# The gate projection of a hybrid decoder layer: 26 of 32 output tiles by seven block products, with gates and branches kept in DRAM

## The chip, the cores and the metric

The kernel runs on one core of a Trainium2 chip. The metric is the device time of one execution in microseconds; the time of a kernel is the median of its runs. The profile is that of one further execution.

## The reference

One layer of a decoder serves 512 prompt tokens and 8 sample tokens (520 in all) with shared weights; `D_MODEL` is 2048. Cut to the part that matters here:

```python
xn = rmsnorm(x, attn_norm_w)
proj = xn @ w_in                                    # q, k, v, gu, gv: 3584 columns
attn = sink_attention(...)                          # 16 heads, window 128 -> 1024 columns
sgu = gelu(gu) * spatial_mix(layernorm(gelu(gv)))   # chunks of 128 positions -> 1024 columns
branch_attn = attn @ w_br_attn                      # 1024 -> 2048
branch_sgu = sgu @ w_br_gm                          # 1024 -> 2048
gates = sigmoid(xn @ w_gate + b_gate)               # 2048 -> 4096
merged = gates[..., D_MODEL:] * branch_attn + gates[..., :D_MODEL] * branch_sgu
x = x + merged @ w_out
# then ConvFFN: up projection 2048 -> 11264, causal conv of width 3, silu gate, down projection 5632 -> 2048
# then x += sigmoid(rmsnorm(x) @ w_ple_gate) * (p @ w_ple_proj)
```

All inputs and outputs are float32.

## The kernel before, in words

Activations lie transposed: a tile holds 128 features by 520 tokens, in two halves of 260 (256 prompt tokens and 4 sample tokens each). A projection works through *n-tiles* of 128 output features; each sums over *k-tiles* of 128 input features. To keep float32 accuracy every operand is split into a rounded part `hi` and a rest `lo`, and a product is taken as hi*hi + hi*lo + lo*hi. A 128x128 block of weights (a *key* `(name, k, n)`) thus costs six matmuls of 260 columns, two halves by three parts (method `mm`).

All weights pass through one stream (`weight_stream`, class `Stream`) whose order is fixed when the program is built. Eight keys make a *block* of 128x1024 that SP loads into a tile `st` (three buffers, three blocks ahead). At the start of block v (`block_start`) ACT casts block v+2 to `hi` (L266) and DVE subtracts it to get `lo` (L273). The other work is hung onto this clock: generators in `self.bg` take one step per block (`tick`), `self.fine` takes one step per key, and `at_block` puts a function at the "snap", "act", "dve" or "end" point of a later block. Each engine runs its instructions in the order in which the program emits them.

The up projection and two of the five chunks of the down projection already use a form with fewer multiplications (`Stream.winograd`, `wpair`): two n-tiles are taken together as a 2x2 block product of (pairs of k-tiles) x (two n-tiles) with the two token halves, and seven products P1 to P7 replace eight. A pair of n-tiles over 16 k-tiles is seven blocks of eight keys, each key costing three matmuls of 260 columns: 168 matmuls for the pair, where the plain form takes 192. The sums of weight blocks are made on the way: tiles `S` and `L` (pool `wsp`) get a second block added by an accumulating DMA from POOL's queue or by DVE (L297, L299). The sums of input tiles are made by `woperands` (`tau`, `X`; ACT casts at L446, DVE subtractions at L449 and sums at L435 to L441), and the seven products are put together again from PSUM with four copies on ACT (L390) and four operations on DVE (L394, L398, L402, L403). In PSUM a phase is either two pairs of banks plus four single banks (plain) or eight single banks (seven products, four for each pair of n-tiles).

Around the change the order is: `front` (normalised input `xn`, input projection, attention on the side), then `gates`, then `w_out`. In `gates` the first loop takes, for each of 16 n-tiles, the attention half of the gate (96 matmuls), multiplies by the row scale `R`, applies the sigmoid, then takes the attention branch `bra` (48 matmuls) and multiplies. Meanwhile the gMLP generator `gmlp` runs one step per block: the GELUs that were left over (L1116), transposes of `gv` (L1154), statistics and scaling per token chunk (L1141 to L1160), the triangular mix of eight channel tiles (L1170 to L1190, matmuls at L1180 and L1181), and last the sample rows (L1194 to L1216, matmuls `gx` at L1211). The second loop takes the other gate half and the branch `brg`, adds, and splits the result into `mg` for `w_out`. `xn` is held as 16 pairs of tiles (hi, lo), each over both token halves. Main storage is a pool of 67 slots of 128x538 floats (`slot`), with a few more slots in phase pools (`extra`).

Of the kernel before, what the change touches and what calls it, by code (L numbers as in the profile page):

```python
# [34 lines left out]
EPS = 1e-6  # L35
SLOT = 538
NSLOT = 67
EARLY_MG = 6
OUT_GROUP = 3
BLK = 8  # L40

# [8 lines left out]
PRODUCTS = ("P1", "P5", "P6", "P2", "P4", "P7", "P3")  # L50
BANK = {"P5": "b", "P1": "a", "P2": "c", "P6": "a", "P4": "d", "P7": "a", "P3": "b"}
KQ = KD // 2

SLOPES = np.exp2(-8.0 * np.arange(1, NH + 1, dtype=np.float32) / np.float32(NH)).astype(np.float32)

# [28 lines left out]
class Stream:  # L84
# [28 lines left out]
    def winograd(self, name, n1, n2, ks):  # L113
        assert not self.open and len(ks) % 2 == 0 and len(ks) <= 2 * BLK
        v = len(self.keys)
        r11, r21, r22, r12 = (self.block([(name, k, n) for k in kk])
                              for kk, n in ((ks[0::2], n1), (ks[0::2], n2), (ks[1::2], n2), (ks[1::2], n1)))
        for p in PRODUCTS:
            self.vblock([(name, p, n1, i) for i in range(len(ks) // 2)],
                        {"P1": ("L", r11), "P7": ("L", r11), "P2": ("st", r12), "P4": ("st", r22)}.get(p, ("S", r21)))  # L120
        acts = self.acts
        acts[v - 6].append(("load", "L", r11, r11))
        acts[v - 1] += [("vsum", "S", r21, ("L", r11)), ("sum", "L", r11, r21)]
        if name == "up":
            acts[v - 9].append(("load", "S", r21, r21))
            acts[v - 8].append(("sum", "S", r21, r22))
            acts[v - 4].append(("load", "st", r12, r12))
            acts[v - 2].append(("load", "st", r22, r22))
            acts[v].append(("vsum", "S", r21, ("st", r12)))
        else:  # L130
            acts[v - 7].append(("load", "S", r21, r21))
            acts[v - 5].append(("load", "st", r22, r22))
            acts[v - 3] += [("vsum", "S", r21, ("st", r22)), ("load", "st", r12, r12)]
            acts[v].append(("vsum", "S", r21, ("st", r12)))
# [8 lines left out]
def weight_stream():  # L143
    o = Stream()
    o.add(paired("in", K_TILES[0], K_TILES[1], KD))
    for n in V_TILES + MIX_TILES:
        o.nt("in", n, range(KD))
    for n in range(KD):
        o.nt("gate", KD + n, range(KD))
        o.nt("bra", n, range(KG))  # L150
    for n in range(KD):
        o.nt("gate", n, range(KD))
        o.nt("brg", n, range(KG))
    for n in range(KD - OUT_GROUP):
        o.nt("out", n, range(KD))
    o.add(grouped("out", range(KD - OUT_GROUP, KD), KD))
    for n in range(KD):
        o.nt("pproj", n, range(KP))
    for j in range(KF):
        o.winograd("up", j, KF + j, range(KD))  # L160
    for c, ks in enumerate(ff_chunks()):
        for n in range(0, KD, 2):
            if seven(c):
                o.winograd("down", n, n + 1, ks)
            else:
                for m in (n, n + 1):
                    o.nt("down", m, ks)
    for n in range(KD):
        o.nt("pgate", n, range(KD))
    return o.done()  # L170
# [13 lines left out]
NCV = _c  # L184


class Kernel:
    def __init__(self, ctx, tc, a):
        self.tc = tc
        self.nc = tc.nc  # L190
        self.a = a
        self.ctx = ctx
        nc = self.nc
        self.stp = ctx.enter_context(tc.tile_pool(name="stp", bufs=3))
        self.sp = ctx.enter_context(tc.tile_pool(name="sp", bufs=NSLOT))
        self.cp = ctx.enter_context(tc.tile_pool(name="cp", bufs=1))
        self.smp = ctx.enter_context(tc.tile_pool(name="smp", bufs=2))
        self.drp = ctx.enter_context(tc.tile_pool(name="drp", bufs=1, space=bass.MemoryType.DRAM))
        self.x1d = [self.drp.tile([128, NT], F32, name=f"x1d{n}") for n in range(KD)]
        self.ppd = [self.drp.tile([128, NT], F32, name=f"ppd{n}") for n in range(KD)]  # L200
        self.fd = [self.drp.tile([128, NT], F32, name=f"fd{j}") for j in range(KF)]
        self.pos = 0
        self.st = {}
        self.hi = {}
        self.lo = {}
        self.bg = []
        self.uid = 0
        self.fine = iter(())
        self.late = defaultdict(list)
        self.slotp = {}  # L210
# [139 lines left out]

    def mm(self, ps, key, x, start, stop):
        whi, wlo = self.wtile(key)
        xh, xl = self.v2(x[0]), self.v2(x[1])
        mm = self.nc.tensor.matmul
        for h in range(2):
            mm(ps[:, h, 0:HW], lhsT=whi, rhs=xh[:, h, :], start=start, stop=False)  # L356
        for h in range(2):
            mm(ps[:, h, 0:HW], lhsT=whi, rhs=xl[:, h, :], start=False, stop=False)  # L358
        for h in range(2):
            mm(ps[:, h, 0:HW], lhsT=wlo, rhs=xh[:, h, :], start=False, stop=stop)  # L360

    def ntile(self, name, n, ks, xs):
        ps = self.mmps()
# [105 lines left out]
    def split(self, src_v, name, scale=None):  # L469
# [9 lines left out]
                                           op0=ALU.mult, op1=ALU.subtract)  # L479
        return hi, lo  # L480

    def rsqrt_rows(self, pss, out, factor, quick=False):

        nc = self.nc
        slow = [] if quick else [None]
        v, y, t = self.slot(name="rv"), self.slot(name="ry"), self.slot(name="rt")
        for h in range(2):
            nc.vector.tensor_scalar(out=v[:, h * HW:(h + 1) * HW], in0=pss[h], scalar1=factor, scalar2=EPS,
                                    op0=ALU.mult, op1=ALU.add)
        nc.vector.reciprocal(y[:, 0:HW], v[:, 0:HW])  # L490
# [46 lines left out]
    def run(self):  # L537
# [40 lines left out]
        with ExitStack() as c1:  # L578
            self.psum(c1, 2, 4)
            with ExitStack() as c2:  # L580
                self.atp = self.phase(c2, "atp")
                self.extra(c2, 8, "s0", "s1", "kT", "sv")
                self.front(x)
            with ExitStack() as c2:
                self.gmp = self.phase(c2, "gmp")
                self.extra(c2, 8, "wt", "nw", "wm", "gnh", "gnl", "mx", "mgx")
                self.gates()
        with ExitStack() as c2:
            self.wsp = self.phase(c2, "wsp", 2)
            with ExitStack() as c1:  # L590
# [19 lines left out]
    def front(self, x):  # L610
# [5 lines left out]
        ps = [self.mmps(), self.mmps()]  # L616

        def xsplit(*ks):
            xn.extend(self.split(self.v2(x[k]), "xn", scale=self.col("an", k)) for k in ks)

        xsplit(0)
        self.split_block(0, (0, 2))
# [65 lines left out]
        self.drain(g4)  # L688
        self.drain(g2)

    def gates(self):
        nc, a, xn = self.nc, self.a, self.xn
        g3 = self.gmlp()
        next(g3)
        self.bg.append(g3)
        merged = []
        for n in range(KD):
            p = self.ntile("gate", KD + n, range(KD), xn)
            m = self.slot(name="mgx" if n < 2 or n >= 10 else "mg")
            nc.vector.tensor_mul(self.v2(m), self.pv(p), self.v2(self.R))  # L700
            nc.scalar.activation(m[:, 0:NT], m[:, 0:NT], AF.Sigmoid, bias=self.col("bg", KD + n))
            p = self.ntile("bra", n, range(KG), self.at)
            nc.vector.tensor_mul(self.v2(m), self.pv(p), self.v2(m))
            merged.append(m)
        self.drain(g3)
        self.sg = [self.split(self.v2(z), "sg") for z in self.gu]
        self.mg = {}
        for n in range(KD):
            p = self.ntile("gate", n, range(KD), xn)
            g = self.slot(name="g")  # L710
            nc.vector.tensor_mul(self.v2(g), self.pv(p), self.v2(self.R))
            nc.scalar.activation(g[:, 0:NT], g[:, 0:NT], AF.Sigmoid, bias=self.col("bg", n))
            if n == KD - 1:
                self.fine = self.split_each(merged, self.mg, EARLY_MG, KD, "mg")
            p = self.ntile("brg", n, range(KG), self.sg)
            nc.vector.tensor_mul(self.v2(g), self.pv(p), self.v2(g))
            nc.vector.tensor_add(merged[n][:, 0:NT], merged[n][:, 0:NT], g[:, 0:NT])
            if n < EARLY_MG:
                self.mg[n] = self.split(self.v2(merged[n]), "mg")
        self.xn = self.sg = None  # L720

    def norm1(self, x):
        nc = self.nc
# [917 lines left out]
```

## Time and profile before

| | |
|---|---|
| median of 3 runs | 2725.32 us (2725.3 to 2725.63) |
| profiled execution | 2725.98 us |
| span of its profile | 2724.3 us, 53560 instructions |
| PE busy | 2707.0 us (99%), 22524 matmuls |
| DVE busy | 1749.6 us (64%) |
| ACT busy | 1196.2 us (44%) |
| POOL busy | 260.7 us (10%) |
| DMA | 390.33 MB, mean 143 GB/s |
| mean granted TensorE clock | 0.999 |

The span is the time from the first to the last instruction of the profiled execution. PE is TensorE's matmuls, DVE is VectorE, ACT ScalarE, POOL GpSimd, SP the engine that issues most transfers. A row of the timeline reads: start, duration, engine, line, operation, output <- inputs, shapes, count, and in brackets how long the engine was idle before it and what released it. A row of the groups by line reads: line, engine, operation, output <- inputs, shapes, count, then busy us and mean ns, then idle time before and its releasers. A row of waits reads: us in total, times, longest. A row of the chain of work that ended last reads: start, duration, piece. Matmuls are pipelined: one is shown with some 280 ns, while they start some 120 ns apart.

### The profile page before, as it was taken

To read this page: it belongs to the slowest core of one execution; us is meant where nothing else is said; L and a number is where in the kernel's file an instruction comes from. 1 tells how busy PE (TensorE), PEld (TensorE's weight loads), DVE (VectorE), ACT (ScalarE), POOL (GpSimd) and SP (SyncE) were. 2 spreads that over 40 slices of the span, in tenths; PEclk is the share of its full clock that TensorE was granted. 3 is DMA by queue.
4 is the path that set the end of the run, shared out by engine and by line. 5 is a ranking of instruction groups with operands and counts; after the bars stand their busy time and mean duration, and the time that the engine had idled before them with its cause. 6 is when DMAs were issued, how large, how long until landed. Compare 5 with 4: busy or idle time off the path is not lost.

```text
span 2724.3 us, 53560 instructions
## 1 busy us (share of the span) xinstructions
PE 2707.0 (99%) x22524; PEld 2703.2 (99%) x22524; DVE 1749.6 (64%) x2594; ACT 1196.2 (44%) x1996; POOL 260.7 (10%) x417
## 2 busy tenths in 40 slices
PE   9999999999999999999999999999999999999999
PEld 9999999999999999999999999999999999999999
DVE  5666555442433343678888888888888677576533
ACT  5365452221322233465555555555556445444321
POOL 0111000000000000011111111111111111110000
PEclk9999999999999999999999999999999999999999
DMA  5223323222222344576666666666658667776343
GB/s 187 92 81 101 102 83 98 89 89 94 88 92 93 94 135 136 162 213 163 178 175 161 177 167 174 172 164 175 173 157 242 158 176 208 158 180 185 112 141 106
DMA packets 129618, 390.33 MB, mean 143 GB/s; under 512 B 14736, under 2 KB 15888, under 8 KB 129376
## 3 DMA queue, kind: packets, MB, share of 16 engines
q1 hardware_dynamic: 101376, 307.75, 34.4%
q0 software_dynamic: 25696, 74.90, 15.6%
q8 instruction: 176, 2.88, 0.4%
q10 hardware_dynamic: 2304, 4.26, 0.4%
q14 instruction: 66, 0.54, 0.1%
HBM read 340.43 MB, written 46.42 MB: 142 GB/s over the span
## 4 chain that ended last, share of the span: by engine, by line
PE 98%; ACT 1%; DVE 1%; DMA 0%; issue 0%; ACTq 0%; SPq 0%; DVEq 0%
PE wa L417 18%; PE mm L356 18%; PE mm L360 18%; PE mm L358 18%; PE wb L417 12%; PE wd L417 6%; PE wc L417 6%; PE po L966 1%; PE s L903 1%; PE pt L948 0%; PE pl L1514 0%; ACT hi L266 0%; DMA ppd<-pp 0%; PE qss L775 0%; ACT pp L1287 0%
## 5 line engine op out<-in xcount | busy, mean ns | idle before, releaser
L273 DVE TENSOR_TENSOR lo<-st,hi 128x1024 fp32r<-128x1024 f32 (+3 forms) x378 | 453.7, 1201 | 376.2 <-ACT hi L266 375.5
L266 ACT CAST hi<-st 128x1024 fp32r<-128x1024 f32 (+3 forms) x378 | 389.6, 1031 | 386.0 <-PE mm L358 149.4
L417 PE MATMUL wa<-X,hi 128*128 128x260 f32 x2736 | 500.6, 283 | 0.9 <-ACT pp L1287 0.9
L417 PEld LDWEIGHTS wa<-X,hi 128*128 128x128 f32 x2736 | 420.8, 188 | 1.1 <-ACT pp L1287 1.1
L356 PE MATMUL mm<-xnh,hi 128*128 128x260 f32 x1920 | 393.9, 287 | 5.6 <-ACT hi L266 5.6
L360 PE MATMUL mm<-xnh,lo 128*128 128x260 f32 x1920 | 386.4, 283 | 0.0
L358 PE MATMUL mm<-xnl,hi 128*128 128x260 f32 x1920 | 386.3, 282 | 0.0
L417 PE MATMUL wa<-X,lo 128*128 128x260 f32 x1368 | 385.7, 282 | 0.0
L417 PE MATMUL wb<-X,hi 128*128 128x260 f32 x1824 | 332.9, 283 | 0.0
L356 PEld LDWEIGHTS mm<-xnh,hi 128*128 128x128 f32 x1920 | 295.4, 189 | 5.7 <-ACT hi L266 5.6
L358 PEld LDWEIGHTS mm<-xnl,hi 128*128 128x128 f32 x1920 | 299.4, 190 | 0.0
L360 PEld LDWEIGHTS mm<-xnh,lo 128*128 128x128 f32 x1920 | 293.5, 188 | 0.0
L417 PEld LDWEIGHTS wb<-X,hi 128*128 128x128 f32 x1824 | 280.5, 188 | 0.0
L266 ACT CAST hi<-S 128x1024 fp32r<-128x1024 f32 (+2 forms) x180 | 181.7, 1009 | 184.5 <-DVE S L299 140.2
L273 DVE TENSOR_TENSOR lo<-S,hi 128x1024 fp32r<-128x1024 f32 (+2 forms) x180 | 210.8, 1171 | 78.5 <-ACT hi L266 78.2
L417 PEld LDWEIGHTS wa<-X,lo 128*128 128x128 f32 x1368 | 257.6, 188 | 0.0
L417 PE MATMUL wb<-X,lo 128*128 128x260 f32 x912 | 256.9, 282 | 0.0
L273 DVE TENSOR_TENSOR lo<-L,hi 128x1024 fp32r<-128x1024 f32 (+2 forms) x120 | 140.7, 1173 | 88.2 <-ACT hi L266 84.2
L417 PEld LDWEIGHTS wb<-X,lo 128*128 128x128 f32 x912 | 172.1, 189 | 0.0
L417 PE MATMUL wc<-X,hi 128*128 128x260 f32 x912 | 166.6, 283 | 0.0
L417 PE MATMUL wd<-X,hi 128*128 128x260 f32 x912 | 166.5, 283 | 0.0
L266 ACT CAST hi<-L 128x1024 fp32r<-128x1024 f32 (+2 forms) x120 | 121.2, 1010 | 100.2 <-PE wd L417 95.5
(297 smaller groups left out, 5246.4 us busy)
## 6 DMA issues: line engine op xcount, KB each, us to landing
st<-in_w SPq DMA_DIRECT2D x343, 512.0 KB, 3.9
S<-in_w SPq DMA_DIRECT2D x44, 512.0 KB, 3.5
S<-in_w POOLq DMA_DIRECT2D x44, 512.0 KB, 7.7
L<-in_w SPq DMA_DIRECT2D x44, 512.0 KB, 3.9
L<-in_w POOLq DMA_DIRECT2D x44, 512.0 KB, 5.5
fd<-hb SPq DMA_DIRECT2D x44, 260.0 KB, 2.2
fr<-fd SPq DMA_DIRECT2D x44, 260.0 KB, 4.9
x1d<-dn POOLq DMA_DIRECT2D x32, 260.0 KB, 5.8
```

The costliest lines, as they stand in the source:

```text
L266: self.nc.scalar.copy(self.hi[v][:, c], self.st[WS.src[v]][:, c])
L273: self.nc.vector.tensor_sub(self.lo[v][:, c], self.st[WS.src[v]][:, c], self.hi[v][:, c].bitcast(F32))
L356: mm(ps[:, h, 0:HW], lhsT=whi, rhs=xh[:, h, :], start=start, stop=False)
L358: mm(ps[:, h, 0:HW], lhsT=whi, rhs=xl[:, h, :], start=False, stop=False)
L360: mm(ps[:, h, 0:HW], lhsT=wlo, rhs=xh[:, h, :], start=False, stop=stop)
L417: nc.tensor.matmul(ps(z), lhsT=w, rhs=x, start=new and i == 0 and q == 0, stop=i == len(X[p]) - 1 and q == 2, skip_group_check=True)
L903: nc.tensor.matmul(out, lhsT=self.cols(q, c), rhs=keys(kk, c), start=n == 0, stop=n == 1)
L966: nc.tensor.matmul(po[:, kb * 128:kb * 128 + w], lhsT=vv[:, kb * 128:(kb + 1) * 128], rhs=pp[:, o:o + w], start=kb == 0 and n == 0, stop=k ...
```

## The change

The stage becomes four:

1. `branch_attn`: the attention branch first, all 16 n-tiles, copied to DRAM (`ad`, issued by ACT). The gMLP generator now runs beside it through `self.fine`, one step every three keys (`paced`). The gMLP's result `gu` is then written to DRAM (`gud`).
2. `gates_plain`: six gate n-tiles in the plain form. Meanwhile `x` is loaded again, scaled, and the operands P4 to P7 of the seven products are built; P1, P2 and P3 use the tiles of `xn` as they are, since `xn` is now split by token halves (`split_halves`, class `Halves`: each tile holds hi and lo of one half).
3. `gates_seven`: the other 26 gate n-tiles as 13 pairs by `wpair`. `gate_end` applies `R`, the sigmoid and, for the attention half, the product with the branch read back from DRAM (`av`), and writes the tile to DRAM (`gd`). During the last pair `gu` is read back and split.
4. `branch_gm`: the gMLP branch, 16 n-tiles; each reads back its two gate tiles, multiplies, adds and splits to `mg`.

```diff
-EARLY_MG = 6
+PLAIN_GATES = 6
+GATE_TILES = tuple(range(KD, 2 * KD)) + tuple(range(KD))
...
-        if name == "up":
+        if name != "down":
...
     for n in range(KD):
-        o.nt("gate", KD + n, range(KD))
         o.nt("bra", n, range(KG))
+    for n in GATE_TILES[:PLAIN_GATES]:
+        o.nt("gate", n, range(KD))
+    for n in range(PLAIN_GATES, 2 * KD, 2):
+        o.winograd("gate", GATE_TILES[n], GATE_TILES[n + 1], range(KD))
     for n in range(KD):
-        o.nt("gate", n, range(KD))
         o.nt("brg", n, range(KG))
...
     def mm(self, ps, key, x, start, stop):
         whi, wlo = self.wtile(key)
-        xh, xl = self.v2(x[0]), self.v2(x[1])
+        if isinstance(x, Halves):
+            xh, xl = [t[:, 0:HW] for t in x.t], [t[:, HW:NT] for t in x.t]
+        else:
+            xh, xl = ([self.v2(t)[:, h, :] for h in range(2)] for t in x)
...
+    def split_halves(self, src, name, scale):
+        nc = self.nc
+        t = [self.slot(F32R, name) for _ in range(2)]
+        for h in range(2):
+            nc.scalar.activation(t[h][:, 0:HW], src[:, h * HW:(h + 1) * HW], AF.Copy, scale=scale)
+        for h in range(2):
+            nc.vector.scalar_tensor_tensor(out=t[h][:, HW:NT], in0=src[:, h * HW:(h + 1) * HW], scalar=scale,
+                                           in1=t[h][:, 0:HW].bitcast(F32), op0=ALU.mult, op1=ALU.subtract)
+        return Halves(t)
...
-    def gates(self):
...
+    def branch_attn(self):
+        nc = self.nc
+        g3 = self.gmlp()
+        next(g3)
+        def paced():
+            for _ in g3:
+                yield
+                yield
+                yield
+        self.fine = paced()
         for n in range(KD):
             p = self.ntile("bra", n, range(KG), self.at)
+            t = self.slot(name="ae")
+            nc.scalar.copy(self.v2(t), self.pv(p))
+            nc.scalar.dma_start(self.ad[n], t[:, 0:NT])
+        self.at = None
+        self.finish_fine()
+        for d in range(KG):
+            nc.sync.dma_start(self.gud[d], self.gu[d][:, 0:NT])
+    def gate_end(self, n, t, b):
...
+        if attn:
+            av = self.slot(name="av")
+            nc.sync.dma_start(av[:, 0:NT], self.ad[i - KD])
+        self.at_block(b, times_r, "dve")
+        self.at_block(b + 1, sigmoid, "act")
+        if attn:
+            self.at_block(b + 2, times_a, "dve")
+        self.at_block(b + 3, lambda: nc.sync.dma_start(self.gd[n], t[:, 0:NT]))
+    def gates_plain(self):
...
+        def run():
+            for i in range(KQ):
+                for k in (2 * i, 2 * i + 1):
+                    xb[k] = self.slot(name="xr")
+                    nc.sync.dma_start(xb[k][:, 0:NT], a["x"][k])
+                yield
+                yield
+                yield
+                yield
+                for k in (2 * i, 2 * i + 1):
+                    nc.scalar.activation(xb[k][:, 0:NT], xb[k][:, 0:NT], AF.Copy, scale=self.col("an", k))
+                yield from build([(p, i) for p in ("P5", "P6", "P4", "P7")], 1)
+        self.fine = run()
+        for n in range(PLAIN_GATES):
+            p = self.ntile("gate", GATE_TILES[n], range(KD), xn)
+            t = self.slot(name="gv")
+            nc.scalar.copy(self.v2(t), self.pv(p))
+            self.gate_end(n, t, 0)
+    def gates_seven(self):
...
+        for n in range(PLAIN_GATES, 2 * KD, 2):
+            if n == 2 * KD - 2:
+                self.fine = sg_parts()
+            c = self.wpair("gate", GATE_TILES[n], GATE_TILES[n + 1], self.X)
+            self.gate_end(n, c["c1"], 1)
+            self.gate_end(n + 1, c["c2"], 2)
+    def branch_gm(self):
...
+        for n in range(KD):
+            load(n + 2)
             p = self.ntile("brg", n, range(KG), self.sg)
+            m, g = gm.pop(n), gg.pop(n)
             nc.vector.tensor_mul(self.v2(g), self.pv(p), self.v2(g))
+            nc.vector.tensor_add(m[:, 0:NT], m[:, 0:NT], g[:, 0:NT])
+            self.mg[n] = self.split(self.v2(m), "mg")
```

More of the change, by code (lines that the diff above doesn't have):

```diff
@@ L184, with __init__ @@
 NCV = _c
+class Halves:
+    def __init__(self, t):
+        self.t = t
 class Kernel:
@@ L199, in __init__ @@
         self.x1d = [self.drp.tile([128, NT], F32, name=f"x1d{n}") for n in range(KD)]
+        self.ad = [self.drp.tile([128, NT], F32, name=f"ad{n}") for n in range(KD)]
+        self.gd = [self.drp.tile([128, NT], F32, name=f"gd{n}") for n in range(2 * KD)]
+        self.gud = [self.drp.tile([128, NT], F32, name=f"gud{n}") for n in range(KG)]
         self.ppd = [self.drp.tile([128, NT], F32, name=f"ppd{n}") for n in range(KD)]
@@ L352, in mm @@
         whi, wlo = self.wtile(key)
-        xh, xl = self.v2(x[0]), self.v2(x[1])
+        if isinstance(x, Halves):
+            xh, xl = [t[:, 0:HW] for t in x.t], [t[:, HW:NT] for t in x.t]
+        else:
+            xh, xl = ([self.v2(t)[:, h, :] for h in range(2)] for t in x)
         mm = self.nc.tensor.matmul
         for h in range(2):
-            mm(ps[:, h, 0:HW], lhsT=whi, rhs=xh[:, h, :], start=start, stop=False)
+            mm(ps[:, h, 0:HW], lhsT=whi, rhs=xh[h], start=start, stop=False)
         for h in range(2):
-            mm(ps[:, h, 0:HW], lhsT=whi, rhs=xl[:, h, :], start=False, stop=False)
+            mm(ps[:, h, 0:HW], lhsT=whi, rhs=xl[h], start=False, stop=False)
         for h in range(2):
-            mm(ps[:, h, 0:HW], lhsT=wlo, rhs=xh[:, h, :], start=False, stop=stop)
+            mm(ps[:, h, 0:HW], lhsT=wlo, rhs=xh[h], start=False, stop=stop)
     def ntile(self, name, n, ks, xs):
@@ L585, in run @@
                 self.gmp = self.phase(c2, "gmp")
-                self.extra(c2, 8, "wt", "nw", "wm", "gnh", "gnl", "mx", "mgx")
-                self.gates()
+                self.extra(c2, 8, "wt", "nw", "wm", "gnh", "gnl", "mx", "ae")
+                self.branch_attn()
+            c2 = ExitStack()
+            self.wsp = self.phase(c2, "wsp", 2)
+            self.extra(c2, 4, "xr", "tau")
+            self.gates_plain()
+        with ExitStack() as c1:
+            self.psum(c1, 0, 8)
+            self.gates_seven()
+        c2.close()
+        self.slotp = {}
+        with ExitStack() as c1:
+            self.psum(c1, 2, 4)
+            self.branch_gm()
         with ExitStack() as c2:
@@ L618, in xsplit @@
         def xsplit(*ks):
-            xn.extend(self.split(self.v2(x[k]), "xn", scale=self.col("an", k)) for k in ks)
+            xn.extend(self.split_halves(x[k], "xn", self.col("an", k)) for k in ks)
         xsplit(0)
@@ L689, in front @@
         self.drain(g2)
-    def gates(self):
-        nc, a, xn = self.nc, self.a, self.xn
+    def branch_attn(self):
+        nc = self.nc
         g3 = self.gmlp()
         next(g3)
-        self.bg.append(g3)
-        merged = []
+        def paced():
[4 more added lines that the diff above has]
+        self.fine = paced()
         for n in range(KD):
[L698 to L701, printed above, removed]
@@ L702, in gates @@
             p = self.ntile("bra", n, range(KG), self.at)
[L703 to L706, printed above, removed]
+            t = self.slot(name="ae")
[5 more added lines that the diff above has]
+            nc.sync.dma_start(self.gud[d], self.gu[d][:, 0:NT])
@@ new lines, in branch_attn, with times_r, sigmoid, times_a @@
+        self.gu = None
+        self.zt = None
+    def gate_end(self, n, t, b):
+        nc = self.nc
+        i = GATE_TILES[n]
+        attn = i >= KD
+        def times_r():
+            nc.vector.tensor_mul(t[:, 0:NT], t[:, 0:NT], self.R[:, 0:NT])
+        def sigmoid():
+            nc.scalar.activation(t[:, 0:NT], t[:, 0:NT], AF.Sigmoid, bias=self.col("bg", i))
+        def times_a():
+            nc.vector.tensor_mul(t[:, 0:NT], t[:, 0:NT], av[:, 0:NT])
+        if attn:
[6 more added lines that the diff above has]
+        self.at_block(b + 3, lambda: nc.sync.dma_start(self.gd[n], t[:, 0:NT]))
@@ new lines, in gates_plain @@
+    def gates_plain(self):
+        nc, a, xn = self.nc, self.a, self.xn
+        X = {p: [None] * KQ for p in PRODUCTS}
+        for i in range(KQ):
+            X["P1"][i] = xn[2 * i].t[0]
+            X["P2"][i], X["P3"][i] = xn[2 * i + 1].t
+        xb = {}
+        self.X, build = self.woperands(xb)
+        self.X.update(X)
+        def run():
+            for i in range(KQ):
+                for k in (2 * i, 2 * i + 1):
[8 more added lines that the diff above has]
+                yield from build([(p, i) for p in ("P5", "P6", "P4", "P7")], 1)
+                del xb[2 * i], xb[2 * i + 1]
+        self.fine = run()
[4 more added lines that the diff above has]
+            self.gate_end(n, t, 0)
+        self.finish_fine()
+        self.xn = None
@@ new lines, in gates_seven, with sg_parts @@
+    def gates_seven(self):
+        nc = self.nc
+        self.sg = {}
+        def sg_parts():
+            raw = {}
+            for d in range(KG + 1):
+                if d < KG:
+                    raw[d] = self.slot(name="gu")
+                    nc.sync.dma_start(raw[d][:, 0:NT], self.gud[d])
+                for _ in range(5):
+                    yield
+                if d:
+                    self.sg[d - 1] = self.split(self.v2(raw.pop(d - 1)), "sg")
+        for n in range(PLAIN_GATES, 2 * KD, 2):
[4 more added lines that the diff above has]
+            self.gate_end(n + 1, c["c2"], 2)
+        self.X = None
+        self.finish_fine()
+        for kind in ("snap", "act", "dve", "end"):
+            self.run_late(kind, self.now())
@@ L707, in gates, with load @@
+    def branch_gm(self):
+        nc = self.nc
+        gm, gg = {}, {}
+        def load(n):
+            if n < KD:
+                for z, i in ((gm, n), (gg, KD + n)):
+                    z[n] = self.slot(name="ml")
+                    nc.sync.dma_start(z[n][:, 0:NT], self.gd[i])
         self.mg = {}
+        load(0)
+        load(1)
         for n in range(KD):
-            p = self.ntile("gate", n, range(KD), xn)
-            g = self.slot(name="g")
-            nc.vector.tensor_mul(self.v2(g), self.pv(p), self.v2(self.R))
@@ L712, in gates @@
-            nc.scalar.activation(g[:, 0:NT], g[:, 0:NT], AF.Sigmoid, bias=self.col("bg", n))
-            if n == KD - 1:
-                self.fine = self.split_each(merged, self.mg, EARLY_MG, KD, "mg")
+            load(n + 2)
             p = self.ntile("brg", n, range(KG), self.sg)
+            m, g = gm.pop(n), gg.pop(n)
             nc.vector.tensor_mul(self.v2(g), self.pv(p), self.v2(g))
-            nc.vector.tensor_add(merged[n][:, 0:NT], merged[n][:, 0:NT], g[:, 0:NT])
-            if n < EARLY_MG:
-                self.mg[n] = self.split(self.v2(merged[n]), "mg")
@@ L720, in gates @@
-        self.xn = self.sg = None
+            nc.vector.tensor_add(m[:, 0:NT], m[:, 0:NT], g[:, 0:NT])
+            self.mg[n] = self.split(self.v2(m), "mg")
+        self.sg = None
     def norm1(self, x):
```

## The prediction, made before the changed kernel was run

> **What bounds the kernel now.** I read the page's first part, then the chain of work that ended last: TensorE carries 98% of it.
>
> ```profile
> span 2724.3 us, 53560 instructions
> PE 2707.0 (99%) x22524; PEld 2703.2 (99%) x22524; DVE 1749.6 (64%) x2594; ACT 1196.2 (44%) x1996; POOL 260.7 (10%) x417
> PE 98%; ACT 1%; DVE 1%; DMA 0%; issue 0%; ACTq 0%; SPq 0%; DVEq 0%
> ```
>
> Then what TensorE waited for in the whole run; these rows are most of it, and 5.6 us of the first is the start:
>
> ```profile
> PE mm L356 <- ACT hi L266: 6.6, 2, 5.6
> PE mm L356 <- ACT pp L1287: 2.0, 3, 0.9
> PE mm L356 <- DVE c L402: 0.6, 1, 0.6
> ```
>
> So time goes with the count of matmuls unless a new wait appears. Busy time by stretch gives the price of one (columns: PE, PEld, DVE, ACT, POOL busy, PEclk, DMA share, GB/s):
>
> ```profile
> 690.00:966.00 276.00, 276.00 (x2302) 276.00 (x2301) 101.39 (x112) 67.90 (x79) 0.00 (x0) 1.00 0.31 96
> ...
> 1235.78:1255.90 20.12, 20.12 (x170) 20.12 (x169) 17.30 (x24) 10.84 (x19) 3.20 (x6) 1.00 0.64 170
> ```
>
> The first is the second gate half with its branch: 16 x (96 + 48) = 2304 matmuls in 276.0 us, 0.1198 us each. The second is one pair of n-tiles by seven products in the up projection. The chain dates a pair by its first block:
>
> ```profile
> 1238.10 2.89 PE wa L417 x24
> ...
> 1258.24 2.89 PE wa L417 x24
> ```
>
> 20.14 us for 7 x 8 x 3 = 168 matmuls, 0.1199 us each: the seven-product form runs at the same rate, TensorE without a gap, at full granted clock. DVE is 17.3 of 20.1 us busy there, so it has room, but little.
>
> **The change part by part.**
>
> *Matmuls (-37.2).* 26 n-tiles leave the plain form: 26 x 96 x 0.1198 = 299.0 us. 13 pairs come: 13 x 20.14 = 261.8 us. The six plain gate tiles, both branches and the gMLP's small matmuls keep their counts. The Trainium skill, "TensorE: Matmul & The Clock Gate", section "Back-to-back issue gap", gives a warm isolated gap of N/2.4 + 2.5 ns; with N = 260 that is 110.8 ns by that page, an estimate that would make this term 312 x 0.1108 = 34.6. The trace disagrees by 9 ns for each matmul, and the trace decides.
>
> *Is the seven-product stage fed?* Groups by line, shapes apart (count, busy us, mean ns):
>
> ```profile
> L273 DVE TENSOR_TENSOR lo<-S,hi 128x1024 fp32r<-128x1024 f32 x132 | 161.6, 1224 | 49.0 <-ACT hi L266 48.9
> L299 DVE TENSOR_TENSOR S<-S,st 128x1024 f32<-128x1024 f32 x44 | 54.2, 1231 | 1.5
> L402 DVE TENSOR_TENSOR c<-wb,un 128x260 f32<-128x260 f32 x60 | 25.3, 421 | 0.0
> L700 DVE TENSOR_TENSOR mg<-mm,R 128x520 f32<-128x520 f32 x8 | 5.6, 700 | 28.4 <-PE mm L360 28.4
> ```
>
> A pair costs DVE seven rests at 1.22, two block sums at 1.23, four combinations at 0.42 and, at most, four products at 0.70 (R and the branch, two tiles): 15.5 us, against 17.3 in the up pair. ACT is below 11. Weight traffic is that of an up pair, 170 GB/s at a DMA share of 0.64; instead of one 266 KB write there are two writes and up to two reads, so about 210 GB/s, share about 0.79. No added wait: I take 0.
>
> *The gMLP mix beside the attention branch alone (+7.6).* Today the generator `gmlp` takes one step per block of 5.76 us. Now `paced` takes one every three keys, 3 x 0.72 = 2.16 us. These rows of today's timeline (PE, ACT, DVE, POOL, and one of the chain) give the chain of work:
>
> ```profile
> 395.34 0.41 PE L356 MATMUL mm<-xnh,hi 128*128 128x260 f32 x2
> ...
> 395.43 8.56 ACT L1116 ACTIVATE z<-z 128x520 f32<-128x520 f32 x16
> 403.88 2.00 ACT L266 CAST hi<-st 128x1024 fp32r<-128x1024 f32 x2
> ...
> 396.15 3.08 DVE L1107 TENSOR_TENSOR al<-ov,ah 64x8 fp32r<-64x8 f32 x16
> 404.95 2.36 DVE L273 TENSOR_TENSOR lo<-st,hi 128x1024 fp32r<-128x1024 f32 x2 [5.72 <-ACT hi L266]
> 407.23 0.69 DVE L1136 TENSOR_TENSOR whl<-wm,whl 128x512 fp32r<-128x512 f32 x1
> 407.83 1.29 DVE L1141 BATCH_NORM_STATS2 sm<-g 128x6 f32<-128x512 f32 x2
> 409.40 0.15 DVE L1145 TENSOR_SCALAR sm<-sm 128x1 f32<-128x1 f32 x1
> 413.04 2.64 DVE L1158 TENSOR_SCALAR z<-g,sm,sm 128x128 f32<-128x128 f32 x8
> ...
> 409.64 0.58 POOL L1147 TENSOR_TENSOR sm<-sm,mhalf 128x1 f32<-128x1 f32 x1 [5.43 <-DVE sm L1145]
> ...
> 401.26 0.87 PE g L1154 x8
> ```
>
> Sixteen GELUs hold ACT to 404.0, so DVE's next rest starts at about 405.0 whatever comes behind it. Then, back to back: rest to 406.2, mask rest to 406.85, and per token chunk 1.3 (statistics) + 0.35 + 0.65 (power on POOL) + 2.64 (eight scalings) = 4.9 us, four times; three rests fall among them (1.14 to 1.2 each, two partly inside the POOL gap): 428.8. Then the first channel tile's product (0.65 net of overlap) and its split on ACT and DVE (0.63 and 0.70, and the handovers):
>
> ```profile
> L475 DVE TENSOR_TENSOR gnl<-z,gnh 128x520 fp32r<-128x520 f32 x8 | 5.6, 700 | 5.6 <-ACT gnh L474 5.6
> L474 ACT CAST gnh<-z 128x520 fp32r<-128x520 f32 x8 | 5.0, 628 | 15.2 <-DVE z L1170 15.2
> ```
>
> That ends at 430.9. TensorE starts the stage at 395.34 and reaches that tile's `mx` matmuls after 34 keys and four transposes: 395.34 + 34 x 0.7195 + 4 x 0.87 = 423.3. It waits 7.6 us in all. The other waits on the way (1 us at the first key for `al`, whose writing ends at 399.2, and PSUM banks of chunks two and three) are parts of it, not added to it. Ends: 0, if DVE should have more room than I count, and 12, with two more rests and two ACT steps of about 1 us in the chain. I take the sum.
>
> After that a channel tile needs about 3.8 us of DVE plus 1.4 of rests in 6.5 + 1.0 us of TensorE: no wait. The last step, the sample rows, had two blocks (11.5 us) and has six keys (4.3 us):
>
> ```profile
> 596.47 0.87 PE g L1194 x8
> ...
> 598.53 1.27 DVE L1141 BATCH_NORM_STATS2 sm<-g 8x6 f32<-8x512 f32 x2
> 603.84 0.61 DVE L1204 TENSOR_SCALAR dgs<-ident,cvt 8x8 f32<-8x8 f32 x4
> ```
>
> 598.53 to 604.45 is 5.9 us of chain: +1.6 (0 to 2.6, with a rest in front as today).
>
> *Operands of the seven products, built in the six plain tiles (0).* Per pair of input tiles, every nine keys (6.5 us): eight 260-wide DVE operations and four casts.
>
> ```profile
> L449 DVE TENSOR_TENSOR X<-xb,X 128x260 fp32r<-128x260 f32 x48 | 18.4, 424 | 2.0 <-ACT X L446 1.9
> L446 ACT CAST X<-xb 128x260 fp32r<-128x260 f32 x48 | 18.0, 408 | 14.6 <-DVE xb L438 6.3 <-DVE xb L441 4.8 <-ACT pp L1287 2.4
> ```
>
> DVE: 8 x 0.42 = 3.4, rests 1.4, gate products 0.8: 5.6 of 6.5 us. ACT: two scalings 1.3, casts 1.6, block casts 1.2, copy and sigmoid 0.7: 4.8. It fits, and casts lead by two blocks (11.5 us), which also covers the `x` reloads at the start of the stage. If DVE and ACT worked by turns, 10.4 - 6.5 = 3.9 us x 8 less 11.5 would be a loss of 20. I take 0: they alternate only inside one operand, and beside the same builder in the w_out stage TensorE lost at most the 2.0 us on `pp` shown above.
>
> *Input held by halves (+0.3).* Two 260-wide operations replace one 520-wide, on ACT and DVE, about 0.1 us per tile (0.41 twice, less the overlap, against 0.65 here); in the first 14 us DVE's rests come just in time, so some 0.3 (0 to 1.5) may show.
>
> ```profile
> 15.74 2.58 ACT L477 ACTIVATE xnh<-x,cvt 128x520 fp32r<-128x520 f32 x4
> ```
>
> *DRAM round trips (0).* SP issues eight `gud`, 32 `gd` writes, 16 `av`, 16 `x`, 8 `gu` and 32 `ml` reads, ACT 16 `ad` writes, all behind matmuls. On SP weight loads queue behind `gd` writes that wait for `times_a`, issued a block later, so they find it done; loads are three blocks early. If a transfer took as long as the longest write on the chain,
>
> ```profile
> 1153.76 6.82 DMA ppd<-pp
> ```
>
> the cover of three short blocks, 8.6 us, still holds.
>
> *PSUM changes (+0.6).* 13 pairs, an odd number, leave the last pair in banks 0 to 3, which `branch_gm`'s first tile takes; it waits for the last combination (L402). The row of 0.6 us above is such a wait. `merged` splits move from the last tile to each tile: hidden.
>
> Sum: -37.2 + 7.6 + 1.6 + 0.3 + 0.6 = -27.1. The profiled execution took 2725.98 us (span 2724.3) and would take 2698.9; the median of the runs is 2725.32, so 2698.2.
>
> **The rivals.**
>
> *A, the sum: 2698* (own range 2692 to 2705).
>
> *B, the pace costs nothing:* DVE gets through before TensorE arrives. 2725.3 - 37.2 + 0.9 = 2689. For: at today's pace DVE is only 65% busy in this stretch. Against: the chain above is serial, nothing in it can be skipped.
>
> ```profile
> 407.00:450.00 43.00, 43.00 (x363) 43.00 (x362) 27.85 (x59) 9.91 (x11) 2.24 (x4) 1.00 0.33 100
> ```
>
> *C, the operand builder overruns:* A plus up to 20, so 2700 to 2718. For: 5.6 of 6.5 us on DVE, engines in order, 64 of 67 slots held by operands, so ACT's eviction may wait for a slot. Against: the 11.5 us lead.
>
> *D, slower, by late accumulating weight loads on POOL's queue:* `L` gets its second block by an accumulating DMA issued a block before the pair and read by the sixth product.
>
> ```profile
> L<-in_w POOLq DMA_DIRECT2D x44, 512.0 KB, 5.5
> ```
>
> It must land within 6 x 2.88 - 1.23 - 1.05 = 15.0 us. To eat 27.1 us over 13 pairs each must be 2.1 us late: landing at 17.1 us or more instead of 5.5. Then 2725 and above. For: DMA share 0.79 instead of 0.64. Against: 44 up pairs lost nothing with the denser DVE. The Trainium skill, "SBUF — State Buffer", section "Who interferes with whom", has a DVE instruction with two SBUF inputs block GpSimd reads, and says that DMAs issued from GpSimd can starve of descriptors under DVE work; by that rule D is the way the change fails. The up stage, with more such DVE work, bears out no delay that reaches TensorE.
>
> *E, it does not do what it says:* matmuls are saved but the short blocks stretch. Excluded by the 20.14 us pair, unless gate pairs differ from up pairs: as D.
>
> **How the numbers follow.** A 0.57, B 0.13, C 0.24, D and E together 0.06. No change means within 0.2%, about 5.5 us, what a measurement of this kernel can tell. The range takes A, B's time and C to two thirds: 2687 to 2714. Faster by over 0.2% (below 2719.9): A, B and all of C, 0.93; within, 0.03; slower, 0.04.
>
> **What would show it.** Right: about 22210 matmuls, gate pairs 20.1 us apart, TensorE waits of 7 to 8 us before the first `mx` matmuls of the attention branch (partly before the `g` transposes), released by DVE, and one of 1 to 2 us before `gx`. No `mm` or `wa` wait in the gates. Wrong: waits of `wa`, `wb` on `hi` from `S` or `L` (D), waits of gate `mm` on `hi` or `lo` among the plain tiles (C), or an attention branch without waits (B).

## The result and the profile after

The changed kernel takes 2703.47 us (median of 4 runs, 2702.04 to 2704.76), the kernel before 2725.47 us in the same comparison: 22.0 us less, ratio 0.9919 with a 95% interval of 0.9902 to 0.9936. The forecast was 2698 us with a range of 2687 to 2714. The direction and the mechanism of the gain were as told; 5 us of it did not arrive. One execution of 5409 us, of ten of the kernel below with a step every two keys, is left out of the medians, and nothing here explains it.

The profiled execution is the fastest of the four (2702.04 us, span 2700.3). First the page's count, busy time and chain:

```profile
span 2700.3 us, 53713 instructions
PE 2673.4 (99%) x22212; PEld 2668.0 (99%) x22212; DVE 1871.6 (69%) x2791; ACT 1287.4 (48%) x2173; POOL 288.4 (11%) x443
...
PE 96%; DVE 2%; ACT 1%; issue 0%; DMA 0%; POOL 0%; ACTq 0%; SPq 0%; DVEq 0%; POOLq 0%
```

22212 matmuls instead of 22524, and 2% of the chain now passes through DVE. Next, what TensorE waited for (us in total, times, longest); rows under 1.5 us that the kernel before has too are left out:

```profile
PE mm L372 <- ACT hi L279: 5.3, 1, 5.3
PE mx L1320 <- ACT gnh L490: 3.7, 1, 3.7
PE mm L372 <- ACT pp L1427: 2.6, 3, 1.4
PE gx L1351 <- DVE dgs L1344: 2.2, 1, 2.2
PE g L1294 <- DVE z L1298: 2.0, 3, 0.8
PE mm L372 <- DVE c L418: 1.5, 2, 0.9
...
PE mm L374 <- DVE al L1247: 0.8, 1, 0.8
PE mx L1321 <- DVE gnl L491: 0.6, 2, 0.4
```

The rows of `mx`, `gx`, `g` and `al` are new, 9.3 us together, and all lie in one stage. Busy time by stage (PE, PEld, DVE, ACT, POOL, then PEclk, DMA share, GB/s), in order: attention branch with the gMLP, six plain gate tiles, thirteen pairs, gMLP branch:

```profile
393.40:515.30 121.90, 112.55 (x892) 110.64 (x891) 74.36 (x158) 39.35 (x57) 11.71 (x24) 0.96 0.41 138
515.30:584.80 69.50, 69.50 (x577) 69.50 (x576) 46.11 (x87) 41.91 (x72) 2.56 (x3) 1.00 0.68 213
584.80:846.30 261.50, 261.50 (x2188) 261.50 (x2187) 186.37 (x210) 130.30 (x177) 20.30 (x24) 1.00 0.72 200
846.30:938.50 92.20, 92.20 (x771) 92.20 (x770) 52.91 (x65) 26.03 (x33) 0.00 (x0) 1.00 0.55 187
```

In the last three TensorE is busy without a gap. In the first it lacks 9.35 us, and its granted clock is 0.96. The whole stretch from the first of these matmuls to the first of `w_out` took 568.4 us before (395.34 to 963.8) and takes 545.0 now (393.44 to 938.46). The part ahead of it became 1.9 us shorter in this execution, the part behind it 1.3 us longer.

The first stage in finer windows shows that the two longest waits are followed by a lower clock. The waits of 0.8 us and less before them are not: from 395 to 427 us the clock is 1.00.

```profile
424.00:430.00 6.00, 1.93 (x14) 1.53 (x13) 4.64 (x11) 1.19 (x3) 1.73 (x2) 0.99 0.32 96
430.00:435.00 5.00, 5.00 (x30) 5.00 (x31) 3.89 (x7) 0.98 (x1) 0.00 (x0) 0.67 0.45 155
435.00:485.00 50.00, 49.78 (x417) 49.57 (x417) 30.73 (x51) 17.11 (x23) 3.79 (x7) 1.00 0.37 125
485.00:497.00 12.00, 9.76 (x76) 9.40 (x74) 9.51 (x19) 1.76 (x3) 1.64 (x3) 0.91 0.26 80
497.00:503.00 6.00, 6.00 (x33) 5.98 (x34) 1.16 (x8) 0.00 (x0) 0.00 (x0) 0.62 0.92 352
```

From 497 to 503 TensorE is "busy" for all 6 us and does 33 matmuls, where an undisturbed stretch of that length holds some 51. Clock lost: 5 x 0.33 + 12 x 0.09 + 6 x 0.38 = 5.0 us. The chain of the same execution shows how it comes about:

```profile
427.78 0.61 DVE z L1310
428.41 0.63 ACT gnh L490
429.07 0.71 DVE gnl L491
429.83 0.42 PE mx L1321
...
431.52 0.54 PE mm L372 x2
432.06 0.43 PE mm L374 x2
...
433.64 0.24 PE mm L376 x2
...
494.26 3.09 PE gx L1351 x16
497.35 0.73 PE mm L372 x2
498.08 0.43 PE mm L374 x2
...
501.87 0.24 PE mm L374 x2
```

After the wait a pair of matmuls takes 0.43 us instead of 0.24, once for about 2 us behind the `mx` matmuls and once, with the `gx` matmuls among them, for about 7 us. That is near half speed. The Trainium skill, "TensorE: Matmul & The Clock Gate", section "What's actually happening", has the clock fall to half after an idle window of about 3.4 us; the first wait (3.7 us in one piece) agrees, the second was only 2.2 us, with the row of 16 small `gx` matmuls (3.1 us) behind it.

The same row stands in the kernel before, where TensorE does not wait for it, and there too the clock fell:

```profile
608.00:618.00 10.00, 10.00 (x72) 9.84 (x71) 3.00 (x10) 1.67 (x2) 0.00 (x0) 0.83 0.22 74
```

### The profile page after: what moved, and what is told of

It reads as the page before. It is cut to its first block, busy times and chain, and to the rows that moved or that the text cites. A ratio compares the mean times of both kernels' runs of the same rounds, so it can differ in the third digit from the quotient of the medians.

```text
span 2700.3 us, 53713 instructions
## 1 busy us (share of the span) xinstructions
PE 2673.4 (99%) x22212; PEld 2668.0 (99%) x22212; DVE 1871.6 (69%) x2791; ACT 1287.4 (48%) x2173; POOL 288.4 (11%) x443
## 4 chain that ended last, share of the span: by engine, by line
PE 96%; DVE 2%; ACT 1%; issue 0%; DMA 0%; POOL 0%; ACTq 0%; SPq 0%; DVEq 0%; POOLq 0%
PE wa L433 22%; PE wb L433 15%; PE mm L372 14%; PE mm L376 14%; PE mm L374 14%; PE wd L433 7%; PE wc L433 7%; PE po L1106 1%; PE s L1043 1%; ACT hi L279 0%; PE pt L1088 0%; PE pl L1654 0%; DVE lo L286 0%; DVE z L1298 0%; ACT z L1256 0%
## 5 line engine op out<-in xcount | busy, mean ns | idle before, releaser
L433 PE MATMUL wa<-X,hi 128*128 128x260 f32 x3152 | 576.6, 283 | 0.9 <-ACT pp L1427 0.9
L433 PEld LDWEIGHTS wa<-X,hi 128*128 128x128 f32 x3152 | 485.5, 188 | 1.1 <-ACT pp L1427 1.1
L433 PE MATMUL wa<-X,lo 128*128 128x260 f32 x1576 | 444.7, 282 | 0.0
L286 DVE TENSOR_TENSOR lo<-S,hi 128x1024 fp32r<-128x1024 f32 (+2 forms) x219 | 258.5, 1180 | 99.9 <-ACT hi L279 99.6
L372 PE MATMUL mm<-xn,hi 128*128 128x260 f32 x1088 | 222.9, 286 | 5.3 <-ACT hi L279 5.3
L376 PE MATMUL mm<-xn,lo 128*128 128x260 f32 x1088 | 219.6, 283 | 0.0
L374 PE MATMUL mm<-xn,hi 128*128 128x260 f32 x1088 | 219.3, 283 | 0.0
L310 POOL DMA_DIRECT2D L<-in_w x73 | 63.3, 867 | 1265.5 <-issue 828.9
L372 PEld LDWEIGHTS mm<-xn,hi 128*128 128x128 f32 x1088 | 168.4, 190 | 5.4 <-ACT hi L279 5.3
L433 PEld LDWEIGHTS wd<-X,hi 128*128 128x128 f32 x1120 | 172.2, 188 | 0.1
L376 PEld LDWEIGHTS mm<-xn,lo 128*128 128x128 f32 x1088 | 168.8, 189 | 0.0
```

The source lines that it names most:

```text
L286: self.nc.vector.tensor_sub(self.lo[v][:, c], self.st[WS.src[v]][:, c], self.hi[v][:, c].bitcast(F32))
L310: self.nc.gpsimd.dma_start(self.st[kind, r][:, c], self.a["w"][src][:, c], accum_op=ALU.add)
L372: mm(ps[:, h, 0:HW], lhsT=whi, rhs=xh[h], start=start, stop=False)
L374: mm(ps[:, h, 0:HW], lhsT=whi, rhs=xl[h], start=False, stop=False)
L376: mm(ps[:, h, 0:HW], lhsT=wlo, rhs=xh[h], start=False, stop=stop)
L433: nc.tensor.matmul(ps(z), lhsT=w, rhs=x, start=new and i == 0 and q == 0, stop=i == len(X[p]) - 1 and q == 2, skip_group_check=True)
```

## The experiments

The theory: DVE's chain for the gMLP is asked for too early (the two waits), and idle TensorE then runs on at a lower clock, which the prediction had not priced. The rival: the waits are hand-overs that would only move, or the loss against the forecast sits in the transfers and the operand building.

### The gMLP's steps paced to DVE

```diff
         def paced():
-            for _ in g3:
-                yield
-                yield
-                yield
+            k = 0
+            for t in [0, 9, 12, 17, 20, 25, 28, 33, 36] + [41 + 9 * d + q for d in range(KG) for q in (0, 3, 6)] + [113, 118, 124]:
+                while k < t:
+                    yield
+                    k += 1
+                next(g3, None)
```

> The changed kernel with the gMLP steps spread over the 128 keys of the attention branch by a list: transposes of a token chunk every 8 keys from key 9 on (instead of every 6 from key 3), channel tiles every 9 keys from key 41, 11 keys instead of 6 between the last transposes and gx. Theory 1 (DVE's chain is asked for too early, and the idle TensorE then runs at a lower granted clock): the attention branch stage, 121.7 us in the changed kernel, falls to 107 to 110 us, mx and gx wait under 1.5 us in all, granted clock 1.00 around the first mx, total 2689 to 2693 us. Rival (the waits come from the hand-over of each step between engines and only move, or the loss against the forecast lies in transfers or operand building): stage above 117 us, total 2699 to 2705 us.

Measured: 2690.67 us (2690.39 to 2691.51), ratio to the kernel before 0.9871 (0.9856 to 0.9886), 12.8 us below the changed kernel. The stage takes 108.4 us (394.89 to 503.32). Busy time in windows of the paced kernel, then the small waits that are left in the stage:

```profile
418.00:430.00 12.00, 12.00 (x103) 12.00 (x102) 10.40 (x26) 2.74 (x4) 1.10 (x2) 1.00 0.37 122
430.00:442.00 12.00, 11.65 (x95) 11.27 (x95) 8.87 (x17) 3.69 (x6) 1.18 (x2) 1.00 0.43 135
490.00:502.00 12.00, 12.00 (x101) 11.67 (x101) 8.37 (x22) 2.69 (x3) 1.64 (x3) 1.00 0.14 48
```

```profile
PE mm L374 <- DVE al L1249: 0.8, 1, 0.8
PE mx L1323 <- DVE gnl L491: 0.6, 2, 0.3
```

Theory 1 holds: only the order in time of the same instructions changed, and in this stage the `mx` and `gx` waits (0.6 us left) and the lower clock are gone. DVE is still at 10.4 of 12 us where it had been the bound, so the cover is thin. This is the fastest version found, faster than both kernels.

### TensorE kept busy in the waits

```diff
             ps = [self.aux("mx") for _ in range(2)]
+            for _ in range(32 if d == 0 else 0):
+                nc.tensor.matmul(ps[0][:, 0:256], lhsT=whl[:, 0:128], rhs=whl[:, 0:256], start=True, stop=True)
...
         p = self.aux("gx")
+        for _ in range(18):
+            nc.tensor.matmul(p[:, 0:256], lhsT=whl[:, 0:128], rhs=whl[:, 0:256], start=True, stop=True)
```

> The changed kernel with matmuls whose results are overwritten, put where TensorE idles: 32 of 256 columns before the first mx, 18 before gx, nothing else moved. They split the wait from the lower clock after it. Theory 1a (the idle time itself brings the lower clock, worth about 1.7 us after the first mx and 2 to 3 us at and after gx): first mx still about 36.4 us after the stage's start, granted clock from then on 1.00, stage 117 to 120 us, total 2 to 4 us below the changed kernel: 2699 to 2701.5 us, and its runs lie closer together than the 2.7 us of the changed kernel's. Rival (the lower clock has another cause, or the small matmuls of gx alone bring it): stage 121 to 123 us, total 2702 to 2705 us.

Measured: 2699.85 us (2697.81 to 2703.82), 3.6 us below the changed kernel, ratio to the kernel before 0.9906 (0.9893 to 0.992). The first `mx` starts 35.6 us after the stage's start, as in the changed kernel (429.09 - 393.44), so the chain on DVE and ACT is what it was; the stage takes 118.6 us. The two places:

```profile
430.00:442.00 12.00, 11.65 (x97) 11.37 (x96) 7.95 (x15) 4.34 (x6) 1.18 (x2) 1.00 0.32 103
490.00:502.00 12.00, 12.00 (x88) 11.78 (x88) 6.29 (x20) 1.65 (x2) 1.64 (x3) 0.86 0.46 162
```

After the first wait the clock stays at 1.00, 0.86 in the changed kernel over the same stretch, so it is the idle time that lowers it there. At `gx` it still falls, though TensorE does not wait: the row of 16 small matmuls stands there, as in the kernel before. The forecast that the clock would be 1.00 from the first `mx` on failed there. The runs did not move closer together, as had been expected (6.0 us apart); that part of theory 1a fell.

### A step every two keys

```diff
             for _ in g3:
                 yield
                 yield
-                yield
```

> The changed kernel with a gMLP step every two keys instead of three: the suspected cost enlarged. Theory 1: the chain on DVE sets the first mx, so it stays 36 to 38 us after the stage's start while TensorE would be there 8 us earlier; waits before the first mx 14 to 17 us, a wait of 1 to 2 us before each further channel tile, gx waits 3 to 4 us; stage 133 to 142 us, total 2714 to 2724 us. Rival (TensorE waits for something that its own place in the order sets, not for DVE's chain): first mx at 26 to 30 us, total within 3 us of the changed kernel.

Measured: 2721.24 us (nine runs, 2719.39 to 2723.34), 17.8 us above the changed kernel. The stage takes about 139 us. The waits:

```profile
PE mx L1319 <- ACT gnh L490: 8.6, 5, 5.8
PE g L1293 <- DVE z L1297: 4.6, 3, 3.8
PE gx L1350 <- DVE dgs L1343: 4.0, 1, 4.0
```

TensorE asks for the first `mx` eight microseconds earlier and gets it 34.6 us after the stage's start (35.6 in the changed kernel): three weight rests of 1.2 us fall into the chain instead of four. A place in TensorE's order does not set it; DVE's chain does. The four later waits of the first row sum to 2.8 us, less than the 1 to 2 us each that were forecast. The waits before the first `mx` sum to about 11 us, less than the 14 forecast; to them comes the lower clock, 0.85 to 0.86 in each 12 us from 406 to 442.

### The two waits one at a time

In the tail-only kernel the list is `[3 * i for i in range(35)] + [114]`; in the head-only kernel it is the paced list with `[113, 116, 119]` at its end.

> The changed kernel with one step moved: gx comes 12 keys after the step before it instead of three, all earlier steps stay. Theory 1 (the two waits add up): gx wait of 2.2 us gone, and the lower clock after it mostly too; first mx still 35 to 37 us after the stage's start with its 3 to 4 us wait; 3 to 5 us below the changed kernel, 2698.5 to 2700.5 us. Rival (the first wait shifts everything and the tail costs nothing of its own): 2702 to 2704 us.

> The list of the paced kernel for all steps up to the last transposes, with the changed kernel's six keys between them and gx. Theory 1: no wait before the first mx, gx wait of 1.5 to 2.5 us and a lower clock after it stay; 3 to 5 us above the paced kernel, 2693.5 to 2695.5 us, and together with the tail-only kernel the gains add up to the 12.8 us of the paced kernel within 2 us. Rival (the two waits are one cost that comes back at the tail): 2698 us or more.

Measured: tail only 2698.6 us, 4.9 us below the changed kernel; head only 2693.3 us, 10.2 us below it and 2.6 us above the paced kernel, just outside its range on the good side. The gains add up to 15.1 us against 12.8 for both together: near the 2 us of tolerance, a little over. So the first wait is worth 8 to 10 us with its clock, the second 3 to 5; they are two costs. In the tail-only kernel the first wait is unchanged (`mx` 3.7 us) and `gx` has none; yet the clock falls after the row of `gx` matmuls (500.0 to 501.7 us), which the forecast had mostly gone:

```profile
503.00:515.00 12.00, 12.00 (x90) 12.00 (x89) 1.33 (x2) 3.21 (x5) 0.00 (x0) 0.86 0.83 281
```

In the head-only kernel `mx` has no such wait, and `gx` has:

```profile
PE gx L1353 <- DVE dgs L1346: 2.3, 1, 2.3
```

### The small matmuls and the clock

The paced kernel with a `yield` after each pair of `gx` matmuls, one pair a key from key 120:

> The paced kernel with the 16 small gx matmuls spread over eight keys instead of in one row. In the kernel before, the row of 1.9 us was followed by about 5 us at the lower clock (granted 0.83 over 608 to 618 us); in the paced kernel's profile it was not. Theory 1b (a row of small matmuls counts as idle time and brings the lower clock in some executions): 0 to 1.5 us below the paced kernel, 2689.2 to 2690.7 us, runs within 1.2 us. Rival (small matmuls cost only their own time): same as the paced kernel within 0.3 us, or slower by the eight interruptions.

Measured: 2700.91 us, 10 us slower than the paced kernel. Neither theory gave that. By starting at key 120 it brought back a wait of 1.5 us, and then this (first the stretch with the wait, then the one after it):

```profile
490.00:502.00 12.00, 10.53 (x75) 9.71 (x74) 7.31 (x15) 2.51 (x3) 1.64 (x3) 0.89 0.14 48
502.00:514.00 12.00, 12.00 (x48) 10.73 (x48) 1.80 (x9) 1.64 (x2) 0.00 (x0) 0.50 0.10 40
```

Twelve microseconds at granted clock 0.50, in the profiled execution; four of the five took 2700.3 to 2701.4 us, one 2695.6. Two more kernels part the wait from the spreading: four groups of four from key 124 on, no wait; and one row at key 120, the wait alone.

> The paced kernel with gx in four groups of four small matmuls, one group a key, from key 124 on: the spreading alone, without the wait of 1.5 us that came back where gx was spread from key 120. Theory 1c (only idle time lowers the clock, and small matmuls among the others then only delay its return): no wait, granted clock 1.00, 2690 to 2692 us. Rival 1d (small matmuls by themselves keep the clock low wherever they stand): granted clock 0.5 to 0.9 over the last 12 us of the stage, 2694 us or more.

> The paced kernel with gx in one row as there, but at key 120 instead of 124: the wait of about 1.5 us alone, without the spreading. Theory 1c: wait of 1 to 2 us, lower clock for some 5 us after it, 2.5 to 5 us above the paced kernel, 2693 to 2695.7 us, so about 6 us of the 10 of the spread kernel came from the spreading after the wait. Rival (the wait alone costs the 10 us): 2699 to 2701 us.

Measured: spreading without wait 2691.99 us (2691.07 to 2694.52), 1.3 us above the paced kernel, with ranges that overlap; wait without spreading 2694.11 us, 3.4 us above it. The stretch after each, spread first, then the early row:

```profile
502.00:514.00 12.00, 12.00 (x102) 11.98 (x102) 2.38 (x9) 1.39 (x3) 0.00 (x0) 1.00 0.91 329
```

```profile
496.00:502.00 6.00, 4.85 (x28) 4.83 (x29) 3.75 (x15) 0.99 (x1) 0.89 (x2) 0.73 0.41 148
502.00:508.00 6.00, 6.00 (x52) 6.00 (x51) 0.00 (x1) 1.65 (x2) 0.00 (x0) 0.99 1.02 348
```

Both times lie in the ranges of theory 1c. After the wait and the row the clock fell; small matmuls strewn after a wait held it down for longer, and strewn without a wait they did no harm in this profile, which is of the fastest of four executions. But that only idle time lowers the clock, and always does, is not borne out. The row of 16 lowered it without a wait in three kernels (the one before, the one with added matmuls, tail only: 0.86 over twelve microseconds each) and not in the paced one, nor in the kernel before with halves (1.00 from 612 to 624 us). And two waits of about 2 us with no small matmuls beside them went different ways. In the paced kernel, far behind the changed stages, one was followed by a lower clock; in the spread kernel without a wait at `gx`, one in the plain gate tiles was not (each wait, then the stretch after it):

```profile
1130.37 0.51 PE L372 MATMUL mm<-ph,hi 128*128 128x260 f32 x2 [1.92 <-ACT pp L1429]
1130.00:1142.00 12.00, 11.60 (x81) 11.39 (x82) 5.64 (x12) 8.32 (x16) 1.75 (x2) 0.86 0.49 157
```

```profile
538.87 0.51 PE L372 MATMUL mm<-xn,hi 128*128 128x260 f32 x2 [2.07 <-ACT hi L279]
538.00:550.00 12.00, 10.61 (x87) 10.41 (x87) 10.56 (x22) 8.55 (x16) 0.00 (x0) 1.00 0.57 177
```

What decides whether a wait or a row of some 2 us lowers the clock is not settled. The second of these waits is also a cost that the changed kernel's profile does not have: ACT waited for a late reload of `x` (5.5 us) and so cast the weights late. It is the sign that the prediction names for rival C, though here a transfer was late and not DVE.

### The halves alone

The kernel before with `split_halves` in place of `split` in `front`, and the changed `mm`.

> The kernel before with one part of the change alone: the normed input split and held by token halves. Forecast of the prediction's step: 0.3 us slower (0 to 1.5), so 2725.5 to 2727 us. Rival (the front of the changed kernel's profile was 1.9 us shorter because of the halves): 2723 to 2724 us. If neither, 2725.3 within 0.5 us, the 1.9 us are differences between executions, such as the moment at which the clock rises.

Measured: 2724.03 us (2722.53 to 2727.48, 11 runs) against 2726.13 us before, ratio 0.9992 (0.9984 to 1.0001). Slower by 0.3 us it is not; a gain of 2 us is likelier than none, but the interval holds both. Where it comes from can be seen but not explained. The same stretch of the second gate half, the kernel with halves, then the one before:

```profile
700.00:958.00 258.00, 258.00 (x2174) 258.00 (x2174) 91.45 (x98) 61.48 (x70) 0.00 (x0) 1.00 0.31 96
```

```profile
700.00:958.00 258.00, 258.00 (x2151) 258.00 (x2150) 89.36 (x95) 59.46 (x66) 0.00 (x0) 1.00 0.31 95
```

Without a wait and at full granted clock, 1% more matmuls pass. The branch tiles in this stretch are faster too (0.710 us for each key instead of 0.721), though their input is not held by halves, so the layout of a matmul's own input is not the whole cause. The profile of the kernel with halves also lacks the 1.7 us that the kernel before loses to the lower clock after its `gx` row, so part of the 2 us may be that and not the halves.

## Why the prediction came out as it did, step by step

- *Matmuls, -37.2:* right. The pairs took 261.4 us (forecast 261.8), the branch behind them 92.2, the six plain tiles 69.8 instead of 69.0, by the wider spacing told below. The Trainium skill's formula ("TensorE: Matmul & The Clock Gate", section "Back-to-back issue gap") would have given an estimate of 34.6; the page gives it for an isolated matmul, not for a stream like this one. The paced kernel, with the same 22212 matmuls and without the two waits, is 35.5 us below the kernel before (2726.13 us in its comparison).
- *The seven-product stage fed, 0:* right, 261.50 busy of 261.50 us, DMA share 0.72 (estimate 0.79).
- *The gMLP mix, +7.6:* right as a wait and in its mechanism. The chain, to the end of the first channel tile's split, was forecast at 35.6 us from the stage's start and took 36.3; the waits of `al`, `g` and `mx` sum to 7.1 us.
- *The sample rows, +1.6:* 2.2 us.
- *The step that was left out:* the speed at which TensorE goes on after a wait. The sum treated idle time as its whole price. The granted clock cost 5.0 us in this stage, against 10 x 0.17 = 1.7 us at `gx` in the kernel before (0.83 from 608 to 618 us): +3.3 net. It could be seen in the profile before, in the row of that stretch shown above. The first loop before took 292.4 us, 184.0 of them for the gate tiles; the remaining 108.4 and the forecast waits of 7.6 and 1.6 make 117.6 for this stage. With 3.3 us for the clock and 0.6 for `gx` that is 121.5; it took 121.7.
- *Operand building, 0:* right, the plain stage has no gap; rival C did not happen in the changed kernel (its sign, 2.6 us of waits, stands in one profile of another kernel, above).
- *Input by halves, +0.3:* the sign was not borne out; the experiment gives -2.1 with an interval that just holds zero.
- *DRAM round trips, 0:* right.
- *PSUM, +0.6:* wrong in place. `branch_gm` starts without a wait (its last `wb` matmul at 846.18 us, its first `mm` at 846.30). The waits on L418 lie in the down projection, where the kernel before lost 1.6 us too (0.6 to the same releaser, 1.0 to ACT's `hi`).
- *Rivals:* B fell with the chain, D and E with the pairs (`L` sums landed in 5.6 us, 5.5 before). The rule that the prediction cites from the Trainium skill, "SBUF — State Buffer", section "Who interferes with whom", did not show as a delay that reached TensorE.

The sum of the forecast, -27.1, lies 5.1 us from the medians' difference and 3.1 from that of the two profiled executions (2725.98 and 2702.04). By stage the profiled executions give, against the forecast: attention branch +4.1, six plain tiles +0.8, pairs -0.4, gMLP branch -0.4 (with the 0.6 that did not come), the part ahead -2.2, the part behind +1.3; the sum is 3.2. So the clock's 3.3 is the largest term, and the part ahead, which came out 1.9 us shorter for no reason that was forecast, hid two thirds of it: that the profiled execution is only 3 us off is partly luck. The other 2 us lie between profiled executions and medians: the changed kernel's profile is of the fastest of its four (1.4 us), that of the kernel before lies 0.5 above its median. The scatter between executions goes with their mean granted clock: the changed kernel has 0.998 at 2702.0 and 2702.6 us and 0.997 at 2704.3 and 2704.8, the kernel with added matmuls 1.000 at 2697.8 and 2698.9, 0.999 at 2700.9 and 0.998 at 2703.8. A clock lower by 0.001 over 2700 us is worth about 2.7 us, an estimate. Why it differs from execution to execution is not explained.

## What to carry to other kernels

Where TensorE is the bound, an interruption can cost twice: the wait itself, and a stretch at the lower clock after it. Here the second part was 1.7 us after a wait of 3.7 us, 3.4 us after one of 2.2 us with a row of small matmuls behind it, more where small matmuls were strewn after it, and nothing after one wait of 2.1 us; so it is a range in a forecast, not a fixed price. Work that is moved beside a shorter stage needs its pace set from the slowest engine of its chain: here a list of step positions that leaves DVE more time was worth 12.8 us, of the 35.5 by which the paced kernel is faster than the kernel before. A share of busy time in the old stage (DVE at 65%) says little of that, since it was read at the old pace.

## What the runs showed of the hardware that was not expected

- After a wait of 1.5 us, pairs of matmuls with 8 columns strewn among full ones held the granted clock at 0.50 for 12 us; without the wait, groups of four strewn likewise left it at 1.00.
- The clock that is lost (length of the stretch times what is missing from 1.00) comes to nearly the same amount again and again: 1.7 us after the first wait (5 x 0.33), after the row in the kernel before (10 x 0.17) and after the 1.9 us wait in the paced kernel (12 x 0.14), 3.4 us at `gx` in the changed kernel (12 x 0.09 + 6 x 0.38), and 8.5 us in the kernel with the pairs strewn (12 us each at 0.89, 0.50 and 0.90): one, two and five times 1.7.
- The spacing of the same 128x128 by 260 matmul is not one number. The kernel before has 0.720 to 0.722 us for each key of six wherever it was looked at. With the input held by halves it is 0.727 in the plain gate tiles of the changed and the paced kernel; in the kernel before with halves it is 0.724 in the first gate half, 0.714 in the second and 0.710 in the branch beside it (2174 against 2151 matmuls in 258 us), and between 0.713 and 0.724 along the front, in nearly the same order in the profiles of the changed kernel, tail only and the kernel before with halves (the paced kernel begins with 0.727 instead of 0.713). It is not the granted clock, which is 1.00 in these stretches. What sets it was not tried.
